# Margins in the plan of a hybrid encoder layer, and another spacing of its weight preparation

## The chip, the core and the metric

The kernel runs on one core of a Trainium2 chip, as one program with one launch. The metric is the time of that program on the device in microseconds (us); less is better. Before the change it is 2629.53 us, the median of three runs (2627.81 to 2630.4). The engines of the core run side by side, each its own queue of instructions in order, and wait for each other through semaphores: TensorE (PE, matrix products into eight PSUM banks), VectorE (DVE), ScalarE (ACT), GpSimd (POOL) and SyncE (SP, which issues most of the DMA transfers and all of the transposing ones).

## The reference

One encoder layer is applied to two requests, of 4096 and of 2048 tokens, 1024 wide, with the same weights.

```python
hn = rms_norm(x, norm_g)
proj = hn @ w_in                                   # 1024 -> 3072
na_q, na_k, na_v, na_g, wq, wk, wv, wg, mq, mg = jnp.split(proj, points, axis=-1)
ya = neighbourhood_attention(qa, ka, va, rpb) * jax.nn.silu(na_g)   # 6 heads, 8 x 16 window on a grid 64 wide
yb = windowed_gqa(qb, kb, vb, sink) * jax.nn.silu(wg)               # 6 heads, |t - s| <= 128
yc = memory_attention(qc, km, vm) * jax.nn.silu(mg)                 # 4 heads over 256 memory tokens
y = jnp.concatenate([ya, yb, yc], axis=-1) @ w_out
return x + y
```

Queries and keys of all three groups are normalised per head before the scores. The inputs are float32.

## The kernel before

Tokens are worked on in **superblocks** of 256 (24 of them: 16 of the first request, 8 of the second), each of two blocks of 128. Every product is made of float16 pairs, a high and a low part of each factor, so one projection of a block onto 384 columns is 24 matrix products (`proj`, L305).

[...] The **first pass** is the neighbourhood attention, the **second** the windowed and the memory attention, and the output projection. For a block of the first pass:

- x is loaded (L507), normalised (L524, DVE) and turned by TensorE in two halves into a PSUM bank each (L534, label `xT`); the halves are stored as float16 pairs (L544 ACT, L549 DVE).
- three projections follow (L308, L309, L311; labels `pga`, `pgb`, `pgv`). Queries and keys go to a float32 buffer and are squared (L672, L673 ACT), summed (L710 DVE), turned into a factor (L315 to L317 POOL) and multiplied by it (L717 DVE, label `nrm`); keys also by their gain (L722 POOL, label `kg`).
- TensorE turns queries (after `nrm`) and keys (after `kg`) into a bank each (L737, label `qT`, two tasks a block).

Then, for each superblock and each of three pairs of heads: scores (L936, label `qk`, into four banks at once), the reading of the four banks with bias and row minimum (L961 DVE, label `ttr`), exponentials (L971 ACT), reciprocal (L977, L978), probabilities as float16 pairs (L997 ACT, L1006 DVE), four transposing DMAs issued by SP (L1017), and the products with the values (L1033, label `pv`).

The PSUM banks are divided: two for projections (`pj`), four for turning and scores (`sc`), two for value products (`po`). A block of scores needs all four of `sc`, a turning one of them.

During the first pass the weights of the second are **prepared** as well, in 24 pieces and twice over: a first time each piece is loaded (L823) and its row maxima are taken (L828 DVE); a second time it is loaded again, split into a float16 pair (L855 ACT, L860 DVE) and stored to DRAM (L867), from where the second pass loads it. Lines L809 and L815 set at which superblock a piece becomes due.

**What sets the order.** No order is written out. All work is added as tasks to a plan (`Plan`, L63), each with an engine, an estimated duration, dependencies, a priority (made of the superblock's number and an offset by label, `SHIFT`), buffers that it takes (`acq`) and gives back (`rel`). `Plan.run` plays the tasks through on estimated times: whenever an engine is free it takes the ready task of least priority whose buffers are there, and the order in which it takes them is the order in which the instructions are issued. The chip then runs each engine's queue in that order at its own times. So an estimate in the plan makes no instruction wait by itself; it decides what stands before what.

A task is ready when its last dependency is done in the plan, or `slack` us after that:

```python
def push(now, t):
    if t.slack > 0:
        at(now + t.slack, READY, t)
    else:
        heapq.heappush(ready[t.eng], (t.prio, t.idx, t))
```

Of the kernel before, what the change touches and what calls it, by code (L numbers as in the profile page):

```python
# [41 lines left out]


class Task:
    __slots__ = ("eng", "dur", "fn", "prio", "lat", "acq", "rel", "nd", "succ", "idx", "label", "slack", "xf", "start", "run", "need")

# [9 lines left out]
TIMES = {"tanh": 0.4, "sg": 0.37, "ev": 0.95, "vl2": 0.235, "red2": 0.9, "r8": 2.85, "nrm2": 1.15, "hi2": 0.89, "lo2": 1.0,  # L58
         "wrcp": 0.275, "mmx": 0.63, "mexp": 1.06, "mrcp": 0.23, "mhi": 0.6, "mlo": 0.86, "ym": 0.37, "yh": 0.34, "yl": 0.37,
         "yw": 0.23, "fin": 0.7}  # L60


class Plan:  # L63
# [11 lines left out]
    def add(self, eng, dur, fn, deps=(), prio=0.0, lat=None, acq=(), rel=(), label="", slack=0.0, xf=0.0):  # L75


        t = Task()
        t.eng = t.run = eng
        t.dur, t.fn, t.prio = TIMES.get(label, dur), fn, prio + SHIFT.get(label, 0.0)  # L80
        t.lat = {"pe": 0.2, "dve": 0.13, "act": 0.13, "pool": 0.16, "free": 0.01}.get(eng, 0.1) if lat is None else lat
        t.acq, t.rel, t.succ = tuple(acq), tuple(rel), []
        names = [a[0] if isinstance(a, tuple) else a for a in acq]
        t.need = tuple((a, names.count(a)) for a in dict.fromkeys(names))
        t.idx, t.label, t.xf, t.slack, t.start = len(self.tasks), label, xf, slack, None
        if label.endswith("T"):
            t.xf *= 1.5
        if eng == "sp" and xf > 0:
            t.dur = (0.63 if label.endswith("T") else 0.45) * round(dur / 0.1)
        ds = [d for d in deps if d is not None]  # L90
        t.nd = len(ds)
        for d in ds:
            d.succ.append(t)
        self.tasks.append(t)
        return t
# [21 lines left out]
    def run(self):  # L117
        avail = self.avail = dict(self.caps)
        ready = {t.eng: [] for t in self.tasks}
        busy = {}  # L120
        ev = []
        seq = 0

        def at(when, kind, t):
            nonlocal seq
            heapq.heappush(ev, (when, seq, kind, t))
            seq += 1

        def push(now, t):
            if t.slack > 0:  # L130
                at(now + t.slack, READY, t)
            else:
                heapq.heappush(ready[t.eng], (t.prio, t.idx, t))
        FREE, DONE, READY, MOVE = range(4)
        for t in self.tasks:
            if t.nd == 0:
                push(0.0, t)
        now = 0.0
        done = 0
        dma_free = 0.0  # L140
        while done < len(self.tasks):
            progress = True
            while progress:
                progress = False
                for e, q in ready.items():
                    if busy.get(e, 0.0) > now or not q:
                        continue
                    skipped = []
                    pick = None
                    while q and pick is None and len(skipped) < 25:  # L150
                        item = heapq.heappop(q)
                        if all(avail[a] >= n for a, n in item[2].need):
                            pick = item[2]
                        else:
                            skipped.append(item)
                    for s in skipped:
                        heapq.heappush(q, s)
                    if pick is None:
                        continue
                    progress = True  # L160
                    self.acquire(pick)
                    pick.start = now
                    self.emit(pick)
                    busy[e] = now + pick.dur
                    at(busy[e], FREE, pick)
                    if pick.xf > 0:

                        at(now + (0.71 if pick.label.endswith("T") else 0.53 if e == "sp" else pick.dur) + 0.65, MOVE, pick)
                        if pick.label.endswith("T"):
                            busy[e] = 1e9  # L170
                    else:
                        at(now + pick.dur + pick.lat, DONE, pick)
            if not ev:
                left = [t.label for q in ready.values() for _, _, t in q][:20]
                raise RuntimeError(f"no progress at {now}: {left} {avail}")
            now = ev[0][0]
            while ev and ev[0][0] <= now:
                _, _, kind, t = heapq.heappop(ev)
                if kind == READY:
                    heapq.heappush(ready[t.eng], (t.prio, t.idx, t))  # L180
                elif kind == MOVE:
                    dma_free = max(now, dma_free) + t.xf
                    at(dma_free + 0.95, DONE, t)
                    if t.label.endswith("T"):

                        busy[t.eng] = max(now, dma_free - 0.9)
                        at(busy[t.eng], FREE, t)
                elif kind == DONE:
                    done += 1
                    self.release(t)  # L190
                if kind == DONE or (kind == FREE and t.xf == 0):

                    for s in t.succ:
                        if (s.eng == t.eng and t.xf == 0) == (kind == FREE):
                            s.nd -= 1
                            if s.nd == 0:
                                push(now, s)
        self.length = now


def build(tc, A, out, seqs):
# [3 lines left out]
    NSB = sum(seqs)  # L205
# [200 lines left out]
    for s in range(len(seqs)):  # L406
        mkv_views(s, one("SM", f"mkvs{s}", [P, 2048], F16))
        for b in range(2):
# [5 lines left out]
                  prio=-18, xf=0.27, label="c")  # L414
    t_gk = pl.add("pool", 1.1, lambda: G.dma_start(out=gam.rearrange("p a d -> p (a d)"), in_=A["k_norm_g"].partition_broadcast(P)),
                  prio=-17, xf=0.27, label="c")
# [29 lines left out]
    for nm, c0, n, src, fl, pr, parts in (("a", 0, 384, w_in, "w1", -29.09, 4), ("b", 384, 384, w_in, "w1", -27.0, 2),  # L446
# [4 lines left out]
        for pt_ in range(parts):  # L451
            ks = slice(nk_ * pt_, nk_ * pt_ + nk_)

            def f_l(ks=ks, c0=c0, n=n, src=src, fl=fl):
                SY.dma_start(out=st[fl + "f"][:, ks, c0:c0 + n],
                             in_=src[P * ks.start:P * ks.stop, c0:c0 + n].rearrange("(k p) c -> p k c", p=P))
            t = pl.add("sp", 0.1, f_l, prio=pr, label="wload", xf=2.2 * n / 384 * nk_ / 4,
                       slack={"v": 12.77, "n": 19.0, "m": 38.18, "b": 5.95}.get(nm, 0.0))
# [13 lines left out]
        t = scale_tasks(nm, g2, g, ts + [tg2_], pr - 30, parts=parts if nm in 'abvnm' else 0)  # L472
# [152 lines left out]
    for bt, nm, kw, nr in (("bA", "A", 32, 11), ("bB", "B", 24, 12)):  # L625
# [5 lines left out]
        t = pl.add("sp", 0.2, f_b, [t_T1], prio=0.9, acq=["pf"], label="bias", xf=3.0)  # L631
# [13 lines left out]
    for gs_ in range(NSB):  # L645
        s, g, n = sbs[gs_]
        for blk in range(2):
# [3 lines left out]
            def xT_alloc(gs_=gs_, blk=blk):  # L651
                if blk == 0:
# [5 lines left out]
                           label="xst", slack=9.0, xf=1.46)  # L658
# [18 lines left out]
            for key, nn, o in (("a", 384, 0), ("b", 384, 384)):  # L677
                t = ([t_xT] + list(t_p.values()))[-1]
                ew = 2 if nb == 0 else NK
                for k0 in range(0, NK, ew):  # L680
# [6 lines left out]
                                  prio=pr - 2, acq=["raw", "sq"] if key == "a" else [], rel=[("pj", key, nb)], label="ev" + key)  # L687
            t_p["v"] = pl.add("pe", 24 * (384 / 2.4 + 2.5) / 1000, mk_pg("v", 384), [t_p["b"]] + t_w["v"],
                              prio=pr, acq=[("pj", "v", nb)], label="pgv")
# [116 lines left out]


    pieces = [(nm, kk) for nm in "tgo" for kk in range(NK)]
    step = max(NSB - 8.5, 0.5) / (2 * len(pieces))  # L809
    prep = {}  # L810
    last = {}
    for ps_ in range(2):
        for i, (nm, kk) in enumerate(pieces):

            k_ = min(int(3.0 + (ps_ * len(pieces) + i) * step), NSB - 1)  # L815
            pr = k_ + 0.8
            n = W2[nm]
            src = A["w_out"][kk * P:(kk + 1) * P, :] if nm == "o" else w_in[kk * P:(kk + 1) * P,
# [828 lines left out]
```

## Time and profile before

| | before |
|---|---|
| runs, median (lowest to highest) | 2629.53 us (2627.81 to 2630.4) |
| the profiled execution | 2628.94 us |
| its span, first to last instruction | 2627.1 us |
| mean granted TensorE clock | 0.988 of full speed |

All times in the following are of that one profiled execution, in us from the start of its span. A row that groups instructions gives the line and engine, the operation, what it writes and reads, their shapes and count, then busy time, and idle time before it with what ended that. In a list of waits stand total us, number of times and the longest. In a row by time the idle time just before an instruction stands in brackets with what ended it. In a row by stretches stand, for each engine, busy us and (x) instructions, then the granted TensorE clock as a share of full speed, the busy share of the 16 DMA engines, and GB/s. Matmuls are pipelined and their ends modelled, so rows of one line overlap a little.

### The profile page before, as it was taken

How to read it: one execution, taken by the hardware profiler on the slowest of the kernel's cores; microseconds unless marked ns; L12 is line 12 of the kernel's file. 1: busy time of each engine (PE TensorE's matmuls, PEld its weight loads, DVE VectorE, ACT ScalarE, POOL GpSimd, SP SyncE). 2: the span in 40 equal slices, each digit the busy share in tenths (PEclk: the TensorE clock that was granted, in tenths of full speed). 3: DMA queues.
4: the chain of work that ended last, by engine and by line, in shares of the span. 5: the costliest groups of instructions: out<-in, count | busy, mean ns of one | idle time of the engine just before them, and what ended most of it. 6: DMA issues, size and time to landing. Idle time of an engine off the chain costs nothing.

```text
span 2627.1 us, 58284 instructions
## 1 busy us (share of the span) xinstructions
PE 2530.8 (96%) x22056; PEld 1589.0 (60%) x22056; DVE 1879.4 (72%) x5283; ACT 1247.3 (47%) x3553; POOL 523.4 (20%) x690
## 2 busy tenths in 40 slices
PE   6999998999999999987999999999999999999999
PEld 3666676666676666654555555555555555555555
DVE  6467776776776676676887777777777867777775
ACT  7455655566665665653444333333333433333432
POOL 2453232424243423220000000010001000000000
PEclk9999999999999999988999999999999999999999
DMA  5477777777979976896666566656655645566554
GB/s 197 150 174 174 164 164 162 169 178 195 190 187 219 208 145 153 172 224 138 146 139 125 120 132 130 129 123 124 127 119 119 131 118 130 127 137 129 123 108 111
DMA packets 732218, 394.56 MB, mean 150 GB/s; under 512 B 645344, under 2 KB 685056, under 8 KB 731296
## 3 DMA queue, kind: packets, MB, share of 16 engines
q1 hardware_dynamic: 718368, 346.59, 61.8%
q0 software_dynamic: 13568, 44.25, 4.7%
q8 instruction: 172, 2.82, 0.5%
q14 instruction: 110, 0.90, 0.1%
HBM read 153.72 MB, written 80.74 MB: 89 GB/s over the span
## 4 chain that ended last, share of the span: by engine, by line
PE 62%; DMA 2%; DVE 1%; SPq 1%; ACT 0%; issue 0%; POOL 0%; DVEq 0%; ACTq 0%; POOLq 0%
PE bank L308 7%; PE bank L1537 6%; PE bank L311 6%; PE bank L309 6%; PE bank L1538 6%; PE bank L1539 6%; PE bank L1241 4%; PE bank L1243 4%; PE bank L1242 4%; PE bank L1278 3%; PE bank L1364 3%; DMA pt<-phl 1%; PE bank L1455 1%; PE bank L1389 1%; PE bank L1033 1%; PE bank L936 1%
## 5 line engine op out<-in xcount | busy, mean ns | idle before, releaser
L308 PE MATMUL bank<-w,xT 128*128 128x384 f16 x1152 | 384.0, 334 | 3.3 <-ACT sq L673 2.2
L309 PE MATMUL bank<-w,xT 128*128 128x384 f16 x1152 | 382.8, 333 | 1.2 <-DVE w L370 1.2
L1329 ACT ACTIVATE pf<-pf,sm 128x384 f32<-128x384 f32 (+1 forms) x288 | 172.6, 599 | 289.1 <-DVE sm L1323 288.6
L1537 PE MATMUL bank<-wo,yT 128*128 128x512 f16 x768 | 291.5, 380 | 0.0
L1538 PE MATMUL bank<-wo,yT 128*128 128x512 f16 x768 | 291.1, 379 | 0.0
L1539 PE MATMUL bank<-wo,yT 128*128 128x512 f16 x768 | 291.1, 379 | 0.0
L315 POOL TENSOR_TENSOR r<-r,wA 128x12 f32<-128x12 f32 x48 | 10.4, 217 | 1275.9 <-DVE r L1194 1275.9
L317 POOL TENSOR_TENSOR r<-r,mhalf 128x12 f32<-128x12 f32 (+1 forms) x100 | 226.5, 2265 | 7.8
L311 PE MATMUL bank<-w,xT 128*128 128x384 f16 x1152 | 211.5, 327 | 0.0
L971 ACT ACTIVATE pf<-pf,sm 128x288 f32<-128x288 f32 (+3 forms) x288 | 155.6, 541 | 88.5 <-DVE sm L961 81.9
L1346 DVE SCALAR_TENSOR_TENSOR phl<-pf,sm,phl 128x384 f16<-128x384 f32 (+1 forms) x288 | 174.4, 606 | 8.6
L1006 DVE SCALAR_TENSOR_TENSOR phl<-pf,sm,phl 128x288 f16<-128x288 f32 (+3 forms) x288 | 152.2, 564 | 29.7 <-ACT phl L997 29.0
L1323 DVE CUSTOM_DVE_ANT_0 pf<-bank,wtab,nsink 128x384 f32<-128x384 f32 (+1 forms) x288 | 162.5, 600 | 6.4 <-PE bank L1278 6.3
L308 PEld LDWEIGHTS <-xT 128*128 128x128 f16 x1152 | 115.2, 100 | 83.8 <-issue 14.3
L309 PEld LDWEIGHTS <-xT 128*128 128x128 f16 x1152 | 115.0, 100 | 75.5 <-issue 9.9
L997 ACT ACTIVATE phl<-pf,sm 128x288 f16<-128x288 f32 (+3 forms) x288 | 144.5, 547 | 31.0 <-DMA pt<-phl 14.7
L311 PEld LDWEIGHTS <-xT 128*128 128x128 f16 x1152 | 113.1, 98 | 75.4 <-issue 1.4
L777 PE MATMUL bank<-xT,wn 128*128 128x256 f16 x576 | 157.3, 273 | 0.3 <-DVE sgn L792 0.3
L779 PE MATMUL bank<-xT,wn 128*128 128x256 f16 x576 | 157.0, 273 | 0.0
L778 PE MATMUL bank<-xT,wn 128*128 128x256 f16 x576 | 157.0, 273 | 0.0
L1177 ACT ACTIVATE raw<-bank 128x448 f32<-128x448 f32 x96 | 47.0, 490 | 221.2 <-PE bank L311 215.9
L1411 ACT ACTIVATE pf<-bank,smm 128x256 f32<-128x256 f32 x192 | 88.2, 481 | 125.3 <-DVE smm L1405 125.3
(281 smaller groups left out, 6063.2 us busy)
## 6 DMA issues: line engine op xcount, KB each, us to landing
xTd<-xT POOLq DMA_DIRECT2D x48, 512.0 KB, 4.3
out<-xr SPq DMA_DIRECT2D x48, 512.0 KB
xx<-in_x_prompt SPq DMA_DIRECT2D x32, 512.0 KB
xr<-in_x_prompt SPq DMA_DIRECT2D x32, 512.0 KB
x<-xTd SPq DMA_DIRECT2D x24, 512.0 KB
w<-xTd SPq DMA_DIRECT2D x24, 512.0 KB
vd<-vhl POOLq DMA_DIRECT2D x48, 192.0 KB, 3.0
va<-vd SPq DMA_DIRECT2D x48, 192.0 KB
```

Of the source, the lines that this page charges most:

```text
L308: T.matmul(ps, xt[:, kk], wh[:, kk, cols], start=(kk == 0), stop=False)
L309: T.matmul(ps, xt[:, kk], wl[:, kk, cols], start=False, stop=False)
L311: T.matmul(ps, xt[:, NK + kk], wh[:, kk, cols], start=False, stop=(kk == NK - 1))
L317: G.tensor_tensor(out=r, in0=r, in1=mhalf[:, 0:n], op=ALU.pow)
L777: T.matmul(pv, wh, x[:, :, kk, :], start=(kk == 0), stop=False)
L778: T.matmul(pv, wh, x[:, :, NK + kk, :], start=False, stop=False)
L1323: V.tensor_tensor_reduce(out=pf[:, 0:nk], in0=bank("sc", "w", u)[:, 0:nk], in1=st["wtab"][:, h, c0:c0 + nk], scale=-1.0, scalar=nsink[:, h ...
L1329: S.activation(out=pf[:, 0:nk], in_=pf[:, 0:nk], func=AF.Exp, scale=-1.0, bias=sm[:, 0:1], accum_out=sm[:, 1:2])
L1346: V.scalar_tensor_tensor(out=phl[:, nk:2 * nk], in0=st["pfw", u][:, 0:nk], scalar=st["smw", u][:, 3:4], in1=phl[:, 0:nk], op0=ALU.mult, op ...
L1537: T.matmul(ps, yT[:, 0, ts_], st["wo0"][:, c, cs], start=(ci == 0), stop=False)
L1538: T.matmul(ps, yT[:, 0, ts_], st["wo1"][:, c, cs], start=False, stop=False)
L1539: T.matmul(ps, yT[:, 1, ts_], st["wo0"][:, c, cs], start=False, stop=(ci == 7))
```

## The change

Three labels get a margin in the plan. A turning of queries or keys (`qT`) and a value product (`pv`) become ready 1.5 us later than their last dependency is done in the plan; a reading of scores (`ttr`) gives its bank back 1.5 us after it is done there. Nothing is added to what the engines do: the number of tasks, their instructions, bytes and buffers are the same.

The preparation of weights is spaced anew. `NSB` is 24 and there are 24 pieces. Before, 48 steps of 15.5/48 of a superblock begin at 3.0; now the first round begins at 2.0 with steps of 18.5/72, and the second round takes two such steps a piece.

```diff
+LATE = {"qT": 1.5, "pv": 1.5}
+KEEP = {"ttr": 1.5}
...
-        t.idx, t.label, t.xf, t.slack, t.start = len(self.tasks), label, xf, slack, None
+        t.idx, t.label, t.xf, t.start = len(self.tasks), label, xf, None
+        t.slack, t.keep = slack + LATE.get(label, 0.0), KEEP.get(label, 0.0)
...
-        FREE, DONE, READY, MOVE = range(4)
+        FREE, DONE, READY, MOVE, GIVE = range(5)
...
+                elif kind == GIVE:
+                    self.release(t)
                 elif kind == DONE:
                     done += 1
-                    self.release(t)
+                    if t.keep > 0:
+                        at(now + t.keep, GIVE, t)
+                    else:
+                        self.release(t)
...
-    step = max(NSB - 8.5, 0.5) / (2 * len(pieces))
+    step = max(NSB - 5.5, 0.5) / (3 * len(pieces))
...
-            k_ = min(int(3.0 + (ps_ * len(pieces) + i) * step), NSB - 1)
+            k_ = min(int(2.0 + (i if ps_ == 0 else len(pieces) + 2 * i) * step), NSB - 1)
```

The lines of the kernel move by 5 to 13 with it: L308, L311, L737, L1033, L1241 before are L320, L323, L749, L1046, L1254 after.

What it does to the order shows on TensorE at two places. The first is a block in the middle of the first pass, the 37th, at 856 to 863 us of the trace of before. The rows are those around its two turnings of queries (the first `ident,raw` row) and keys (the second), before:

```order
L311 MATMUL bank_63<-w_307,xT 128x384
L737 MATMUL bank_68<-ident,raw 128x2x4x16 x3
L737 MATMUL bank_65<-ident,raw 128x128 x3
L1033 LDWEIGHTS va
L1033 MATMUL bank_69<-pt,va 64x8x16
```

and after, where the dots stand for the rest of a value product and of a projection:

```order
L323 MATMUL bank_64<-w_307,xT 128x384
L749 MATMUL bank_65<-ident,raw 128x2x4x16 x3
L1046 LDWEIGHTS va
L1046 MATMUL bank_69<-pt,va 64x8x16
...
L320 MATMUL bank_63<-w_307,xT 128x384
...
L323 MATMUL bank_63<-w_307,xT 128x384
L749 MATMUL bank_66<-ident,raw 128x128 x3
```

The keys' turning has moved behind the value product and a whole projection; the queries' turning stands where it stood.

The second place is the end of the first pass on TensorE, from its last scores (`ring,qT`, 64x256) to the first gates of the second pass (the row that reads `x_15604,wn` or `x_15572,wn`). Projections of the second pass write 128x448. Shown is the first product of each group, before:

```order
L936 MATMUL bank_66<-ring,qT 64x256
...
L308 MATMUL bank_63<-w_16526 128x448
...
L1033 MATMUL bank_69<-pt,va 64x8x16
...
L308 MATMUL bank_64<-w_16526 128x448
...
L1033 MATMUL bank_70<-pt,va 64x8x16
...
L1241 MATMUL bank_64<-x_15604,wn_16898 128x256
```

Here one projection, one value product, two projections and three value products lie between the last scores and the gates. After:

```order
L949 MATMUL bank_65<-ring,qT 64x256
...
L320 MATMUL bank_63<-w_16407 128x448
...
L1046 MATMUL bank_69<-pt,va 64x8x16
...
L1254 MATMUL bank_63<-x_15572,wn_16788 128x256
...
L1046 MATMUL bank_70<-pt,va 64x8x16
...
L1254 MATMUL bank_63<-x_15572,wn_16788 128x256
```

The last scores are now followed by two projections and three value products; then come two gates, the last value product, and further gates. One projection has moved ahead of the last scores.

More of the change, by code (lines that the diff above doesn't have):

```diff
@@ L44 @@
 class Task:
-    __slots__ = ("eng", "dur", "fn", "prio", "lat", "acq", "rel", "nd", "succ", "idx", "label", "slack", "xf", "start", "run", "need")
+    __slots__ = ("eng", "dur", "fn", "prio", "lat", "acq", "rel", "nd", "succ", "idx", "label", "slack", "xf", "start", "run", "need", "keep")
 SHIFT = {"bE": 0.02, "c": 1.22, "eva": 0.26, "evb": -0.01, "exp": -0.1, "g2": 1.94, "hi": 0.3, "kg": -1.0,
```

## The prediction

> **What bounds the kernel now.** First the page as a whole: the span, the share of each engine, and the strips of the span in 40 slices.
>
> ```profile
> span 2627.1 us, 58284 instructions
> PE 2530.8 (96%) x22056; PEld 1589.0 (60%) x22056; DVE 1879.4 (72%) x5283; ACT 1247.3 (47%) x3553; POOL 523.4 (20%) x690
> ...
> PE   6999998999999999987999999999999999999999
> ...
> PEclk9999999999999999988999999999999999999999
> DMA  5477777777979976896666566656655645566554
> ```
>
> TensorE has work for 2530.8 of 2627.1 us and the next engine, VectorE, for 1879.4. So the end is set by TensorE's own matmuls plus the 96.3 us in which it stands idle, and only those 96 us (and time at a lower clock) can be won by another order. The next view, the busy time in four stretches, says where they are.
>
> ```profile
> core 0: us, PE busy (x) PEld busy (x) DVE busy (x) ACT busy (x) POOL busy (x), PEclk, DMA share, GB/s
> 0.00:150.00 150.00, 122.83 (x759) 78.53 (x760) 81.83 (x197) 84.93 (x167) 61.66 (x91) 0.97 0.50 169
> 150.00:1140.00 990.00, 947.97 (x10891) 659.55 (x10890) 700.03 (x1868) 604.85 (x1572) 332.67 (x459) 0.99 0.80 178
> 1140.00:1230.00 90.00, 67.35 (x561) 44.47 (x560) 57.63 (x170) 34.73 (x109) 13.87 (x15) 0.85 0.80 189
> 1230.00:2627.00 1397.00, 1392.66 (x9851) 806.50 (x9847) 1039.93 (x3049) 522.84 (x1707) 115.20 (x126) 1.00 0.59 126
> ```
>
> Idle are 27.2 us in the start, 42.0 us in the first pass (neighbourhood attention), 22.6 us at the hand-over to the second pass, and 4.3 us in all 1397 us after it. The second pass is full: nothing is to be had there, and its order changes only in its first superblocks. The list of who waited for whom on TensorE names the 42.0 us of the first pass:
>
> ```profile
> PE bank L1033 <- DMA pt<-phl: 12.9, 9, 3.7
> PE bank L534 <- DVE sm L961: 10.4, 6, 3.5
> PE bank L737 <- POOL raw L722: 6.8, 6, 2.2
> PE bank L737 <- DVE raw L717: 6.3, 6, 3.1
> ...
> PE bank L936 <- DVE xT L549: 1.6, 2, 1.3
> PE bank L737 <- DVE sm L961: 0.8, 1, 0.8
> ```
>
> The columns are total us, times, and the longest. Value products (L1033) wait 12.9 us for turned probabilities; the turning of queries and keys (L737) waits 13.9 us in 13 places for their norm and gain; the turning of x (L534) waits 10.4 us and scores (L936) 1.6 us for a score bank.
>
> A wait costs more than its length, because the clock halves after it. Five stretches of the granted clock (the third number from the right):
>
> ```profile
> 189.50:192.90 3.40, 3.40 (x43) 1.94 (x43) 2.14 (x5) 2.60 (x6) 1.32 (x2) 0.50 0.88 271
> 404.50:407.90 3.40, 3.40 (x13) 1.95 (x14) 2.13 (x6) 3.40 (x9) 0.00 (x0) 0.50 0.13 26
> 452.30:455.70 3.40, 3.40 (x16) 2.77 (x16) 1.97 (x8) 3.40 (x10) 0.00 (x0) 0.50 0.83 135
> 810.70:817.50 6.80, 5.44 (x50) 3.13 (x50) 3.65 (x6) 3.37 (x6) 5.55 (x8) 0.50 1.15 295
> 861.90:865.30 3.40, 3.40 (x40) 2.27 (x40) 2.80 (x6) 1.85 (x5) 3.20 (x7) 0.50 0.89 149
> ```
>
> At 0.50 each 3.4 us do the work of 1.7. These five lose 10.2 us, and the mean of 0.99 over 990 us agrees with about 10. Two of them (404, 452) follow waits of L534, two (189, 810) waits of L1033, one (861) a wait of L737.
>
> **The margin at queries and keys.** The stretch at 856 us shows what is to be removed: two turnings back to back, each late.
>
> ```profile
> 856.75 1.46 PE L311 MATMUL bank<-w,xT 128*128 128x384 f16 x8
> 858.75 0.55 PE L737 MATMUL bank<-ident,raw 128*128 128x128 f32 x3 [0.54 <-DVE raw L717]
> 861.42 0.55 PE L737 MATMUL bank<-ident,raw 128*128 128x128 f32 x3 [2.12 <-POOL raw L722]
> 861.90 1.49 PE L1033 MATMUL bank<-pt,va 128*64 128x128 f16 x32
> ```
>
> The first order excerpt shows this place: after the change a value product (1.49 us here) and a projection stand between the two turnings. The projection's length is in the next fence: 448.00 - 444.09 = 3.91 us. So the second turning comes 5.4 us later in TensorE's work and its wait of 2.12 us is covered. In all 48 blocks the pair is now split by at least one other piece of work (41 were back to back). Counted over the rows of the order at lengths like these, the first turning stands at least 8.0 us of work behind the projection it needs, where it stood 7.5 at the least. The waits for POOL's gain (6.8 us) should nearly all go. Of the 7.1 us for VectorE the longest, 3.1, can lose only about 1.5. I take 10 of 13.9 us; the bounds are 4 (the margin is eaten by later norms) and 13.9.
>
> **The margin at value products.** 12.9 us in 9 waits is 1.4 us in the mean, longest 3.7. A product that comes 1.5 us later clears the mean wait and leaves 2.2 of the longest. But scores are pushed back as well, so the work between a pair's scores and its product grows in some places and shrinks in others. I take 8 of 12.9; bounds 0 and 12.9.
>
> **The margin at score banks.** It clears L936: 1.6 us. For L534 I take nothing of 10.4 us. These rows of TensorE and VectorE show why:
>
> ```profile
> 443.13 1.02 PE L936 MATMUL bank<-ring,qT 64*64 64x256 f16 x48
> 444.09 0.34 PE L308 MATMUL bank<-w,xT 128*128 128x384 f16 x1
> ...
> 448.00 0.60 PE L534 MATMUL bank<-ident,xx 128*128 128x128 f32 x4
> 452.12 1.19 PE L534 MATMUL bank<-ident,xx 128*128 128x128 f32 x5 [3.52 <-DVE sm L961]
> ...
> 403.17 0.82 DVE L828 TENSOR_REDUCE sc_gmx<-xw 128x1 f32<-128x640 f32 x1 [5.97 <-DMA xw<-in_w_in]
> ...
> 450.41 1.22 DVE L828 TENSOR_REDUCE sc_omx<-xw 128x1 f32<-128x1024 f32 x1 [4.37 <-DMA xw<-in_w_out]
> 451.55 0.51 DVE L961 CUSTOM_DVE_ANT_0 pf<-bank,bA 128x352 f32<-128x352 f32 x1
> ```
>
> VectorE stood 4.37 us before a weight maximum (L828) whose load had not landed, and the scores' reading (L961), which frees the bank, was queued behind it; the row at 403 is the same ahead of the half-clock stretch at 404. Scores and turning of x lie one projection (3.91 us) apart, and in the new order they mostly still do; 1.5 us more in the plan was already inside that distance. What could end this wait is another place of the maximum, which the new step gives, by luck. Bounds 0 and 10.4.
>
> **The clock.** With those waits the half-clock stretches at 189, 810 and 861 should mostly go: 1.7 + 3.4 + 1.7 = 6.8 us. I take 4, bounds 0 and 10.2. [...]
>
> **The weight step.** Pieces of the first pass over the later weights come every 18.5/72 = 0.26 superblocks instead of 15.5/48 = 0.32, those of the second every 0.51 instead of 0.32. No instruction and no byte is added. When the largest pieces of the second pass are split shows in this row (ns shortest/median/longest, then first and last start in us):
>
> ```profile
> L855 ACT ACTIVATE xhl<-xw,sc_ogs x8: 1132/1148/1150, 792.0 to 917.6; 128x1024 f16<-128x1024 f32 x8
> ```
>
> That is where the DMA strip has its two 9s side by side (788 to 919 us); these pieces come half as often there now. Its gain is contained in the L1033 term; alone I price it at 0. Bounds: minus 5 (waits like that at 452 are gone) to plus 10 (the denser maxima make two more, each 3.5 us and 1.7 of clock).
>
> **The hand-over.** Here the change can cost. Waits between 1140 and 1230 us, and the end of the first pass on TensorE:
>
> ```profile
> PE bank L1033 <- DMA pt<-phl: 8.8, 4, 4.4
> PE bank L1364 <- DMA pt<-phl: 4.4, 3, 2.7
> PE bank L1389 <- DVE sm L1323: 4.1, 3, 2.0
> ...
> 1136.60 1.68 PE L311 MATMUL bank<-w 128*128 128x448 f16 x8
> 1141.57 1.68 PE L311 MATMUL bank<-w 128*128 128x448 f16 x8
> 1143.18 0.95 PE L1033 MATMUL bank<-pt,va 128*64 128x128 f16 x33
> 1148.48 0.77 PE L1033 MATMUL bank<-pt,va 128*64 128x128 f16 x16 [4.36 <-DMA pt<-phl]
> ```
>
> Before, three projections of the second pass lay between the last scores and the last value products; now two (second order excerpt). One such projection is 1141.57 - 1136.60 = 4.97 us here, gap-free. The first of the last products meets its probabilities that much earlier, and nothing is late behind it but the other products. Against this, two gates are put ahead of the very last product. Scores and mask work of the second pass are also re-ordered up to about its fourth superblock. I take plus 5; bounds minus 5 (the gates cover it) and plus 15 (the whole of it, again at half clock as PEclk 0.85 shows for this stretch).
>
> **Sum.** 10 + 8 + 1.6 + 4 - 5 = 18.6 us off. The profiled execution took 2628.94 us (span 2627.1 and 1.8 around it), 0.6 under the median of 2629.53. 2628.9 - 18.6 = 2610.
>
> **The rivals.**
> - *All waits go* (chance 0.08). Also those for a bank, and the hand-over stays as it is: 42.0 + 10.2 = 52 us at most, less what starts anew; about 2585. For it: every wait of the first pass is at one of the three places or comes from a bank. Against: the bank waits come from late loads.
> - *The clock does not come back* (0.05). The waits shrink but the rest is enough to halve the clock as often: 2628.9 - 14.6 = 2614. [...]
> - *The waits only move* (0.22). An order has no time in it: scores are pushed back as well, and what stood before a product stands before the next scores. For it: between scores and product the work is the same in many superblocks. The change does not do what it says, within 8 us of 2626; a third of it faster by over 0.2%.
> - *Slower at the hand-over* (0.14). The last products run into their probabilities, 5 us each for the last two, and into the first window products (L1364 and L1389, 8.5 us now), which stretches the half clock as well. It decides from the point where the hand-over loses more than the first pass wins: at the lower bounds that is 4 + 1.6 won against 10 and some 4 of half clock lost, 2628.9 + 8.4 = 2637.
> - *The denser maxima* (0.07). The step of 0.26 superblocks makes VectorE wait for loads more often just ahead of a scores' reading. Two of 24 reach TensorE now; at six it is 4 x (3.5 + 1.7) = 21 us against 18.6: 2631.
>
> **How the numbers follow.** Forecast 0.44, all waits 0.08, clock 0.05, move 0.22, hand-over 0.14, maxima 0.07. A measurement of this kernel can tell about 0.2%, 5.3 us, from no change. Faster by more: 0.44 + 0.08 + 0.05 and a third of 0.22, 0.64. Slower by more: the hand-over and some of the maxima and the moves, 0.20. Within: 0.16. The range for 8 in 10 leaves out most of "all waits" below and the worst of the hand-over above: 2588 to 2637.
>
> **What would show it.** In the first pass the waits of the turning of queries and keys for POOL fall below 2 us and for VectorE below 3; those of the value products for turned probabilities to about 5; the bank waits of x stay, but at other times, each behind a weight maximum on VectorE; half-clock stretches fall to two or three. Between the end of the first pass and the first output product the idle time rises by about 5 us. The DMA strip has no 9 near 850 us. The forecast is wrong if the idle time of the first pass stays above 35 us, or if the hand-over loses over 15.

## Result and profile after

| | before | after |
|---|---|---|
| median | 2629.53 us | 2651.94 us |
| lowest to highest | 2627.81 to 2630.4 | 2645.99 to 2655.26 |
| ratio of after to before (95% interval) | | 1.0083 (1.0069 to 1.0097) |
| profiled execution, its span | 2628.94, 2627.1 us | 2645.99, 2644.2 us |

The change made the kernel 22.4 us slower; 2610 was forecast, and the range ended at 2637. The profiled execution of after is the lowest of its runs, so the traces show 17.1 us of the difference. Of the experiments below, one execution of e8_tenth (6069 us) and one of h1_pool_before (2926 us) were far slower than all others; the ratios leave them out, and without them the two medians are 2633.74 and 2613.05 us.

The page of after, answering to the first fence of the prediction:

```profile
span 2644.2 us, 58237 instructions
PE 2536.9 (96%) x22056; PEld 1593.6 (60%) x22056; DVE 1878.6 (71%) x5283; ACT 1247.6 (47%) x3553; POOL 524.1 (20%) x690
...
PE   6999988999999999987999999999999999999999
...
PEclk9999999999999999988999999999999999999999
DMA  5466977887888986886766656665555645566654
```

TensorE's work is the same 22056 matmuls. Its busy time grew by 6.1 us, about what the longer time at half clock makes of the same work (worked out below), and its idle time by 11.0 (from 96.3 to 2644.2 - 2536.9 = 107.3). The busy time by stretches says where (us of the stretch, then busy us of each engine, then clock); the stretches end some 15 us later than those of before, as the work does:

```profile
0.00:150.00 150.00, 123.77 (x745) 79.28 (x746) 82.35 (x196) 86.81 (x170) 61.84 (x94) 0.97 0.50 171
150.00:450.00 300.00, 273.94 (x3063) 191.99 (x3061) 203.82 (x540) 165.62 (x437) 96.98 (x137) 0.97 0.78 165
450.00:750.00 300.00, 288.17 (x3480) 202.61 (x3479) 219.69 (x584) 191.50 (x483) 93.93 (x131) 0.99 0.86 181
750.00:1155.00 405.00, 391.92 (x4399) 269.50 (x4398) 277.90 (x749) 246.95 (x649) 144.09 (x191) 0.98 0.86 178
1155.00:1250.00 95.00, 69.32 (x551) 45.24 (x551) 58.67 (x175) 35.91 (x118) 11.19 (x13) 0.82 0.69 175
1250.00:2644.00 1394.00, 1389.73 (x9826) 804.95 (x9824) 1036.13 (x3045) 520.86 (x1700) 116.09 (x126) 1.00 0.59 127
```

The first pass (150 to 1155) idles 51.0 us where it idled 42.0; the hand-over 25.7 where it idled 22.6; start and second pass are as before. Of the first pass the stretch from 150 to 450 took nearly all: 26.1 us of idle time. In before it is this row, with 14.4:

```profile
150.00:450.00 300.00, 285.61 (x3329) 200.97 (x3327) 215.84 (x580) 179.83 (x477) 99.74 (x142) 0.98 0.77 168
```

The waits of TensorE in the first pass of after:

```profile
PE bank L1046 <- DMA pt<-phl: 18.0, 8, 6.3
PE bank L362 <- DVE sc_gis L356: 7.0, 1, 7.0
PE bank L949 <- DVE xT L561: 5.1, 9, 1.2
PE bank L749 <- DVE sm L974: 4.1, 3, 2.1
PE bank L749 <- DVE raw L729: 4.1, 3, 2.6
...
PE bank L949 <- DVE ring L315: 2.2, 2, 1.5
PE bank L362 <- DVE sc_tis L356: 2.2, 1, 2.2
PE bank L546 <- DVE sm L974: 1.5, 1, 1.5
PE bank L546 <- DVE ring L315: 0.9, 1, 0.9
PE bank L749 <- POOL raw L734: 0.9, 2, 0.6
```

The waits at the turning of queries and keys (L749) and of x (L546) are shorter. But those of value products (L1046) are longer, scores (L949) wait for other things than before, and a line that had no wait in the first pass of before stands second: L362, the small product that makes the scale of a weight out of its maxima. The two longest waits, by time, with what stood before them on SP and VectorE:

```profile
303.14 2.83 SPq L816 DMA_DIRECT2D va<-vd  x4
306.01 8.50 SPq L1030 DMA_TRANSPOSE pt<-phl  x2
...
318.38 2.08 PE L1046 MATMUL bank<-pt,va 128*64 128x128 f16 x47 [6.25 <-DMA pt<-phl]
...
347.91 2.63 SPq L816 DMA_DIRECT2D va<-vd  x4
350.64 0.46 SPq L836 DMA_DIRECT2D xw<-in_w_in  x1
...
360.13 0.82 DVE L841 TENSOR_REDUCE sc_gmx<-xw 128x1 f32<-128x640 f32 x1 [7.08 <-DMA xw<-in_w_in]
...
361.41 0.58 PE L362 MATMUL bank<-sc_gis,ones 128*128 128x1 f32 x2 [6.96 <-DVE sc_gis L356]
```

At 303 four value loads (L816) went out ahead of the turnings of probabilities; two of those took 8.50 us on SP (a median one takes 1.29), and the product behind them was 6.25 us late. At 360 VectorE stood 7.08 us before a weight maximum whose load had not landed, and TensorE with it; that load (L836, at 350.64) had been issued right behind four more value loads. Half clock stands at both, 6.8 and 10.2 us of it:

```profile
316.40:323.20 6.80, 4.82 (x99) 3.98 (x99) 1.62 (x4) 0.92 (x2) 0.00 (x0) 0.50 1.07 311
357.40:367.60 10.20, 6.19 (x21) 3.15 (x22) 6.20 (x29) 3.46 (x10) 0.00 (x0) 0.50 0.57 93
...
862.50:869.30 6.80, 6.12 (x32) 3.15 (x32) 3.84 (x10) 3.37 (x9) 3.97 (x6) 0.50 0.98 237
...
sum 37.40, PE 30.04 PEld 18.07 DVE 19.54 ACT 15.37 POOL 11.40; mean PE 4.29 PEld 2.58 DVE 2.79 ACT 2.20 POOL 1.63
```

The sum is that of all seven half-clock stretches of the first pass; before, there were 23.8 us (the five that the prediction showed, and 3.4 us at 322.6), with TensorE at work for 22.4 of them. VectorE's waits for the loads of the weight maxima grew as well, from 32.4 us (11.6 + 11.4 + 9.4) to 56.0:

```profile
DVE sc_gmx L841 <- DMA xw<-in_w_in: 20.7, 4, 9.4
DVE sc_tmx L841 <- DMA xw<-in_w_in: 20.6, 6, 8.4
DVE sc_omx L841 <- DMA xw<-in_w_out: 14.7, 4, 5.4
```

### The profile page after: what moved, and what is told of

Same layout as the page of the kernel before. It is cut to its first block, busy times and chain, and to the rows that moved or that the text cites. A ratio compares the mean times of both kernels' runs of the same rounds, so it can differ in the third digit from the quotient of the medians.

```text
span 2644.2 us, 58237 instructions
## 1 busy us (share of the span) xinstructions
PE 2536.9 (96%) x22056; PEld 1593.6 (60%) x22056; DVE 1878.6 (71%) x5283; ACT 1247.6 (47%) x3553; POOL 524.1 (20%) x690
## 4 chain that ended last, share of the span: by engine, by line
PE 58%; DVE 2%; DMA 1%; ACT 1%; POOL 0%; issue 0%; SPq 0%; DVEq 0%; ACTq 0%; POOLq 0%
PE bank L1550 6%; PE bank L1551 6%; PE bank L1552 6%; PE bank L320 6%; PE bank L321 6%; PE bank L323 6%; PE bank L1254 4%; PE bank L1256 4%; PE bank L1255 4%; PE bank L1291 3%; PE bank L1377 3%; PE bank L1468 1%; PE bank L1402 1%; DMA pt<-phl 1%; PE bank L1046 0%
## 5 line engine op out<-in xcount | busy, mean ns | idle before, releaser
L320 PE MATMUL bank<-w,xT 128*128 128x384 f16 x1152 | 384.9, 335 | 3.4 <-ACT sq L685 3.1
L323 PE MATMUL bank<-w,xT 128*128 128x384 f16 x1152 | 213.3, 329 | 0.0
L1019 DVE SCALAR_TENSOR_TENSOR phl<-pf,sm,phl 128x288 f16<-128x288 f32 (+3 forms) x288 | 157.2, 583 | 23.3 <-ACT phl L1010 22.4
L320 PEld LDWEIGHTS <-xT 128*128 128x128 f16 x1152 | 115.6, 100 | 82.3 <-issue 14.7
L323 PEld LDWEIGHTS <-xT 128*128 128x128 f16 x1152 | 113.9, 99 | 77.4 <-issue 4.5
```

Source lines behind the costliest of these rows:

```text
L320: T.matmul(ps, xt[:, kk], wh[:, kk, cols], start=(kk == 0), stop=False)
L323: T.matmul(ps, xt[:, NK + kk], wh[:, kk, cols], start=False, stop=(kk == NK - 1))
```

## The experiments

All of them compute the same as the kernel before. "Step" is the new spacing of the weight pieces, "margins" the other two edits. Ratios are to runs of the kernel before on the same chip.

| label | what it is | median us | ratio (95% interval) |
|---|---|---|---|
| e1_step_only | new step, no margin | 2637.72 | 1.0023 (1.0013 to 1.0033) |
| e2_margins_only | margins, old step | 2649.26 | 1.0067 (1.0047 to 1.0088) |
| e3_scale_margin | after, and L362 8 us later in the plan | 2658.36 | 1.0103 (1.0084 to 1.0121) |
| e4_no_bank_margin | old step, two margins (no bank margin) | 2657.99 | 1.0097 (1.0075 to 1.0119) |
| e5_bank_only | old step, bank margin alone, 0.8 us | 2654.01 | 1.0088 (1.0072 to 1.0105) |
| e6_value_only | old step, value margin alone | 2635.58 | 1.0022 (1.0012 to 1.0032) |
| e7_turn_only | old step, margin of queries and keys alone | 2642.14 | 1.0047 (1.0032 to 1.0062) |
| e8_tenth | old step, all margins 0.1 us | 2635.35 | 1.0020 (1.0009 to 1.0031) |
| f1_loads_spread | after, value loads among the turnings | 2664.69 | 1.0136 (1.0119 to 1.0154) |
| f2_maxima_later | after, maxima later on VectorE | 2637.17 | 1.0024 (1.0009 to 1.0039) |
| f3_both_after | f1 and f2 together | 2656.45 | 1.0106 (1.0080 to 1.0132) |
| f4_both_before | the same two on before | 2696.82 | 1.0261 (1.0236 to 1.0285) |
| g1_maxima_before | before, maxima later | 2614.26 | 0.9934 (0.9918 to 0.9951) |
| g2_maxima_margins | e2, maxima later | 2642.23 | 1.0042 (1.0027 to 1.0056) |
| g3_maxima_value | e6, maxima later | 2615.49 | 0.9939 (0.9925 to 0.9954) |
| g4_loads_on_pool | after, value loads issued by POOL | 2628.75 | 0.9999 (0.9985 to 1.0013) |
| h1_pool_before | before, value loads issued by POOL | 2613.07 | 0.9940 (0.9924 to 0.9955) |
| h2_pool_maxima_before | before, both moves | 2615.94 | 0.9953 (0.9936 to 0.9971) |

### The parts of the change

The first runs take the change apart. e1 keeps the new step and empties the tables of margins; e2 does the opposite:

```diff
-LATE = {"qT": 1.5, "pv": 1.5}
-KEEP = {"ttr": 1.5}
+LATE = {}
+KEEP = {}
```

> The new step of the weight preparation alone, no margin anywhere. Theory A (the step loses the time: its denser maxima stop VectorE for loads, and the scale product L362 on TensorE waits behind them, 7.0 + 2.2 us and 10.2 us of half clock in the changed kernel): 2645 to 2660, with waits of L362 for sc_gis or sc_tis on TensorE. Theory B (the margins lose it, by putting scores and value products in worse places): within 5 us of 2629.5.

> The three margins alone, with the old step. Theory A: 2610 to 2625, waits of L749 and L1046 in the first pass shorter than before, no wait of L362 for sc_gis. Theory B: 2640 to 2655, with waits of L1046 and L949 as in the changed kernel.

The step alone cost 8 us and the margins alone 19 (8 + 19 = 27 against 22 together): both parts cost, and the margins more. e2 lies in the range of theory B, e1 between the two theories. e2 shows where the margins lose: its value products wait longer than in before, although each has a margin of 1.5 us.

```profile
PE bank L1046 <- DMA pt<-phl: 21.8, 10, 6.9
PE bank L749 <- DVE raw L729: 14.5, 8, 5.0
```

e3 is after with the scale product held back in the plan, for the wait of 6.96 us:

```diff
-LATE = {"qT": 1.5, "pv": 1.5}
+LATE = {"qT": 1.5, "pv": 1.5, "sc2": 8.0}
```

> The changed kernel, and in the plan the scale product of a weight (sc2, L362) becomes ready 8 us later, so that other work stands before it on TensorE. If its waits and the half clock behind them are 14 us of the loss, as the trace of the changed kernel adds up (9.2 us of waits and 10.2 us at half clock): 2634 to 2642, no wait of L362 for sc_gis or sc_tis above 1 us. If these waits only show a late VectorE that something else would meet: no change, 2646 to 2655, with the wait at another line.

The wait went and the kernel became 6 us slower still, which neither theory had: one number in the plan had drawn the whole order anew. So taking a wait out by a margin does not test what that wait costs. e4 leaves out the margin at score banks (`KEEP = {}`, old step):

> Old step, margins at the turning and at value products only, none at score banks. If the bank margin is what pushes scores back: waits of L949 for VectorE as before the change (1.8 us) and a time below the margins alone by 3 us or more. If it is harmless: within 4 us of the margins alone.

Value products then waited only 9.0 us, but the kernel lost 28, more than either theory allowed. Next, each margin alone, and all of them at a length that can cover nothing (old step in all four):

```diff
e5  +LATE = {}                         +KEEP = {"ttr": 0.8}
e6  +LATE = {"pv": 1.5}                +KEEP = {}
e7  +LATE = {"qT": 1.5}                +KEEP = {}
e8  +LATE = {"qT": 0.1, "pv": 0.1}     +KEEP = {"ttr": 0.1}
```

> The old weight step; of the three margins only the one at score banks, at 0.8 us instead of 1.5 (with 1.5 alone the plan finds no order). Theory 'lead': bank waits fall a little, scores are pushed back, shortest distance to the value product stays 14.5; 2627 to 2637. Theory 'redrawn': 2635 to 2660.

> The old weight step; of the three margins only the one at value products (1.5 us). In the written order the work between a pair's scores and its value product grows to 21.4 us in the mean and 17.9 at the least (before 20.0 and 14.3; with all margins 20.0 and 15.4), since nothing pushes the scores back. Theory 'lead': the margin at value products fails in the full change because the other margins push the scores back as far; alone it works, so the first-pass waits of value products for turned probabilities fall from 12.9 to about 5 us and the time is 2615 to 2628 us. Theory 'redrawn': any order other than that of before meets new waits, the size of a margin decides nothing; the waits of value products fall, others rise by as much or more, and the time is 2635 to 2660.

> The old weight step; of the three margins only the one at the turning of queries and keys (1.5 us). Theory 'lead': the second turning moves from 10.3 to 13.1 us behind its projection, the 13.9 us of waits there fall below 4, but scores go back and value products lose lead (shortest 13.9 us): their waits rise from 12.9 to about 25; 2630 to 2640. Theory 'redrawn': 2635 to 2660, with the new waits at places that have no margin in common (score banks, weight maxima, value products).

> The old weight step; all three margins at 0.1 us instead of 1.5, which is too short to cover any wait of a microsecond or more. The written order is redrawn all the same: the second turning of queries and keys stands 11.9 us behind its projection (before 10.3, with 1.5 us 13.8). Theory 'lead' (margins of 1.5 us do the harm, by their size): within 5 us of before, 2625 to 2635. Theory 'redrawn' (the order of before is a fortunate one, any other costs): as the full margins, 2637 to 2660.

By their times, "lead" fell at e5, e6 and e7, where "redrawn" was right in sign and size; e8 came out at the edge of "lead", 0.2% (5 us) above before. One mark of "lead" did come in e7: value products waited 23.8 us, where it had about 25. Margins of 0.1 us, which cover no wait of a microsecond, cost 5 us; one margin alone costs 5, 12 or 24, all three 19, and two of them 28. What an order costs does not follow the size or the number of the margins. The value margin alone did at its place what it was to do, and this is what stood there then (first-pass waits of e6):

```profile
PE bank L546 <- DVE sm L974: 11.7, 7, 3.7
PE bank L949 <- DVE sm L974: 6.4, 3, 5.6
PE bank L1046 <- DMA pt<-phl: 5.0, 3, 2.3
PE bank L749 <- DVE sm L974: 4.9, 3, 2.0
PE bank L949 <- DVE xT L561: 3.8, 6, 1.3
```

The waits of products went from 12.9 to 5.0 us as hoped, and TensorE's waits for VectorE from 19.9 to 34.4 (all rows of that list together).

### The two queues, without a new order

To see what single waits cost, the other runs keep the plan's order and move a few instructions when they are issued. f1 issues the four value loads one behind each of the next four turnings; f2 issues each weight maximum up to eight pieces of VectorE's work later:

```diff
 # f1
     def emit(self, t):
+        if t.label == "vld":
...
+            self.hold = [lambda cb=cb: t.fn(cbs=[cb]) for cb in range(4)]
+            return
         t.fn()
+        if t.label == "pT" and self.hold:
+            self.hold.pop(0)()
 # f2
     def emit(self, t):
+        if t.label == "wpm":
+            self.hold, self.left = [t.fn], 8
+            return
+        if self.hold:
+            self.left -= t.eng == "dve"
+            if self.left == 0 or t.label in ("wpl", "sc1"):
+                self.hold.pop()()
         t.fn()
```

> The full change, its order kept on every engine; only the four value loads of a superblock (L816), which stand together on SP, are issued one behind each of the next four turnings of probabilities. Theory 'queue': the long waits of the full change for turned probabilities (6.3, 3.3 and 2.6 us at 312, 985 and 860 us) arise because the turnings stand behind those loads on SP; they go, the first-pass waits there fall from 18 to about 8, and with the half clock behind them the time falls by 10 to 16 us, to 2636 to 2642. Theory 'only moves': the turnings are as late as before for other loads, or another engine is late next; within 5 us of 2652.

> The full change, its order kept on every engine but VectorE, where each weight maximum (L841) stands up to eight pieces of work later. Theory 'queue': VectorE waits 56 us for loads of the maxima, with the readings of scores queued behind; this falls below 25, TensorE's first-pass waits for VectorE fall from 28 to about 15 us, and the time falls by 8 to 18 us, to 2634 to 2644. Theory 'only moves': the waits on VectorE shrink but TensorE's waits for it stay above 23 us; within 5 us of 2652.

> The full change with both: value loads one behind each turning, and the maxima up to eight pieces later on VectorE. Theory 'queue': the two add up, 2618 to 2634, so most of what the change lost is regained without touching a margin. Theory 'only moves': 2640 to 2657.

> The kernel before (old step, no margin, its order), with the value loads one behind each turning and the maxima up to eight pieces later on VectorE. Theory 'queue': of the first pass's 42 us of waits those behind value loads (3.8 us at 807) and behind maxima (L534, 10.4 us) go, with some half clock; 2612 to 2624. Theory 'fortunate order': before has few such meetings to lose, and the moved pieces make new ones; 2625 to 2640.

f2 fits "queue" by its time: VectorE's waits for these loads fell from 56.0 to 9.2 us, and 15 us were gained. TensorE's waits for VectorE fell from 28.1 to 19.3 us, less than it asked, and the wait at the scale product stayed (7.0 us in after, 6.7 in f2). f1 went the wrong way. Its wait of 6.25 us was gone, but products now waited for the loads themselves, which they had done in neither kernel (f1, then f4):

```profile
PE bank L1056 <- DMA pt<-phl: 15.9, 12, 3.8
PE bank L1056 <- DMA va<-vd: 8.9, 5, 3.3
```

```profile
PE bank L1064 <- DMA pt<-phl: 38.0, 26, 4.4
PE bank L1064 <- DMA va<-vd: 24.6, 18, 3.4
```

f4 and g1 below differ in the place of these loads alone: 2696.82 against 2614.26, so that place is worth 83 us there. On the changed order it cost 13 us (f1) and 19 us (f3 against f2). f1, f3 and f4 thus say that the meeting of loads and turnings on SP matters, not that it made the difference. The next runs apply each move to both kernels; g4 and h1 take the loads off SP altogether:

```diff
-                SY.dma_start(out=va[0:4 * kw, cb, :], in_=vsrc[:, CB_KC0[cb]:CB_KC0[cb] + kw, :])
+                G.dma_start(out=va[0:4 * kw, cb, :], in_=vsrc[:, CB_KC0[cb]:CB_KC0[cb] + kw, :])
```

> The kernel before, its order kept on every engine but VectorE, where each weight maximum stands up to eight pieces of work later. VectorE's waits for the loads of the maxima fall from 32 to below 8 us. Theory 'maxima': the re-drawn order made these waits reach TensorE, while in the order of before they mostly did not; so the gain here is small, 0 to 7 us, 2622 to 2631. Theory 'common cost': both kernels have it and the difference of 22 us stays; the gain is as in the full change, 12 to 17 us, 2613 to 2619.

> All three margins of 1.5 us, the old weight step, and each weight maximum up to eight pieces later on VectorE. Without the last it took 2649. Theory 'maxima': VectorE's 45 us of waits for loads go below 15, and the time comes to 2629 to 2638. Theory 'redrawn': value products wait 21.8 us here for turned probabilities, with which the maxima have nothing to do; 2642 to 2650.

> Only the margin at value products, the old weight step, and each weight maximum up to eight pieces later. Without the last it took 2636, its value products waiting 5 us instead of 12.9 and VectorE making TensorE wait 34 us instead of 20. Theory 'maxima': the 34 us fall to about 18 and the margin's own gain shows: 2612 to 2622, below the kernel before. Theory 'redrawn': 2628 to 2638.

> The full change, its order kept; only the value loads (L816) are issued by POOL instead of SP, at the same place of the order. Theory 'queue': the waits of value products behind such a load (6.3, 3.3 and 2.6 us at 312, 985 and 860 us) go; POOL issues for some 4 us more in each superblock and its gain (L734) comes later, which the margin at queries and keys covers; 2638 to 2646. Theory 'only moves': the turnings are as late as before, or the gain makes the turning of queries and keys wait 10 us or more; 2647 to 2665.

> The kernel before, its order kept; only the value loads are issued by POOL instead of SP. In the full change this took 23 us off. Theory 'loads': the re-drawn order put value loads right ahead of turnings that TensorE waits for, the order of before mostly not (one long wait, 3.8 us at 807, stands behind one); the gain here is 0 to 8 us, 2623 to 2631, and the two kernels come within 5 us of each other. Theory 'common cost': 15 to 25 us are gained here too, 2606 to 2616, and the change stays about 20 us slower with the loads away. Theory 'gain late': without the margin at queries and keys POOL's issuing makes the turning wait for the gain, from 6.8 us up to 15 or more; 2631 to 2645.

> The kernel before with both moves: value loads issued by POOL, and each weight maximum up to eight pieces later on VectorE. The maxima alone took it to 2614. If the two add up, with 0 to 8 us from the loads, 2606 to 2614; with a common cost of the loads of 15 to 25 us, 2590 to 2600; if POOL's gain is late instead, 2615 to 2630.

**The maxima** are a common cost: moving them gave 17 us on before and 15 on after, and the gap between the two stayed at 2637.17 - 2614.26 = 22.9 us. g2 gained 7 of the 11 to 20 that "maxima" asked and lies in the range of "redrawn". g3 landed where "maxima" had put it, but not for its reason: it and g1 differ in the value margin alone and came out 1.2 us apart, within the spread of either. With VectorE's waits for the loads of the maxima gone (0.6 us in g1, 32.4 before), that margin is worth nothing, and its order, which cost 5 us in e6, costs nothing either.

**The loads on SP** were worth 23 us on after and 16 on before, so by the medians they too are mostly a common cost, as one theory had it; g4 came out faster than both of its theories allowed. The gap between the two kernels fell from 22.4 to 15.7 us, by about as much as the intervals of the four ratios leave open. The traces of one execution each say where the rest is. The stretches of g4, then of h1:

```profile
150.00:1130.00 980.00, 949.60 (x10938) 663.34 (x10937) 704.47 (x1868) 604.88 (x1566) 395.25 (x547) 0.99 0.86 180
1130.00:1230.00 100.00, 71.29 (x599) 46.62 (x594) 61.20 (x185) 38.16 (x124) 11.18 (x13) 0.81 0.71 172
```

```profile
150.00:1125.00 975.00, 944.80 (x10900) 659.12 (x10898) 704.31 (x1868) 606.28 (x1573) 394.99 (x547) 0.99 0.81 181
1125.00:1215.00 90.00, 68.98 (x574) 45.44 (x573) 59.24 (x179) 35.36 (x112) 13.63 (x15) 0.85 0.80 192
```

Idle in the first pass are 30.4 and 30.2 us: the 9.0 us by which the changed order idled more are gone. The half clock of the first pass is equal too, 20.4 us in each. Most of what is left of the gap (2623.1 - 2610.2 = 12.9 us of span) is the hand-over: 28.7 us idle against 21.0, and 37.5 us of half clock against 27.3. So on these two traces the loss of the first pass arises only together with the value loads on SP, and the loss at the hand-over does not. With the maxima moved instead, the first passes stay apart (f2 idles 995 - 951.8 = 43.2 us there, g1 978 - 945.2 = 32.8).

The waits did not simply go where "queue" had put them. At the three products that it named, 6.25, 3.25 and 2.61 us of after became 3.15, 3.95 and 0.62 in g4, so only some of that waiting hangs on the place of the value loads. The wait at L362 fell from 7.0 to 0.9 us, though nothing was moved on VectorE: the weights' loads stand on SP as well, and VectorE's waits for them fell from 56.0 to 39.2 us in g4, and from 32.4 to 12.5 in h1. In h1 the waits of value products hardly changed (12.9 to 11.9 us); there the turning of x (10.4 to 6.2) and of queries and keys (13.9 to 9.6) waited less. By which step on the way that happens was not tried.

The best are h1 and g1, both on the kernel before, at 2613 and 2614 us (0.6% below it). The two moves do not add up: h2 took 2616. Its waits for POOL's gain are only 3.5 us, so that theory is not the reason; h1 alone had already taken most of VectorE's waits for the maxima away, which fits that the second adds nothing; it was not tried further.

## Why the prediction was wrong

Its account of the first pass, against what after shows (us of waits before and after; a change below zero is a gain):

| step | forecast | before, after | change |
|---|---|---|---|
| turning of queries and keys, L737/L749 | -10 | 13.9, 9.1 | -4.8 |
| value products, L1033/L1046 | -8 | 12.9, 18.0 | +5.1 |
| scores, L936/L949 | -1.6 | 1.8, 7.6 | +5.8 |
| turning of x, L534/L546 | 0 | 10.4, 2.4 | -8.0 |
| scale products, L350/L362 | none | 0, 9.2 | +9.2 |
| projections and gates | none | 2.6, 4.0 | +1.4 |
| sum of waits | -19.6 | 41.6, 50.3 | +8.7 |
| half clock, half of TensorE's work in it | -4 | 11.2, 15.0 | +3.8 |
| hand-over, idle and half clock | +5 | | +5.5 |

For the last row: idle +3.0, and TensorE's work in the half-clock stretches from 16.8 to 21.8 us, half of which is 2.5. Half, because the 128x384 products of a projection start 0.32 us apart in the half-clock stretch at 404.5 of before (405.58, 405.90) and 0.16 us apart right behind it (408.05, 408.21). The prediction took half of the whole length of such stretches (10.2 us in five of them); where TensorE idles within one, as at 810, that counts the idle time twice. Counted as in the table, the rows sum to 8.7 + 3.8 + 5.5 = 18.0 us; 0.9 is won in the start, which leaves the 17.1 us of span.

- **The step that failed** is the sum itself: "10 + 8 + 1.6 + 4", rows of the old order's list of waits taken off its time. Off the waits and the half clock of the first pass 23.6 us were to come; 12.5 were added. A margin in this plan does not take a wait out; it draws another order for all engines, which meets waits of its own. The nearest rival, "the waits only move", named this, but priced it at no change. The runs show that the moves were not neutral: nine redrawn orders (after, and e1 to e8) all came out slower, by 5 to 28 us. That the order of before is a fortunate one fits this; why no redrawn one was better is not shown.
- *Queries and keys.* Right for POOL (6.8 to 0.9, "below 2" was asked), wrong for VectorE (7.1 to 8.2, "below 3").
- *Value products.* Wrong in sign in the full change, right alone: the margin took 7.9 us off in e6 for a forecast of 8. With this margin and none at score banks the products waited 5.0 and 9.0 us (e6, e4), with both margins 21.8 and 18.0 (e2, after). The count ahead of e6 fits that: the work between a pair's scores and its product is 20.0 us in the mean before, 21.4 with the value margin alone, and 20.0 again with all three, so the other margins take back what this one gives. The prediction had named this ("scores are pushed back as well") and still took the 8.
- *Turning of x.* Said to stay "each behind a weight maximum", gained by luck; it waits 8.0 us less in after, and f2 and g1 show that the place of the maxima was worth 15 to 17 us. I had taken that as out of reach of the change and priced it at zero.
- *Weight step.* Priced at 0 with bounds of -5 and +10; e1 measured +8. Of the DMA strip's pair of 9s one is gone; the other stays in the slice from 859 to 925 us, where none was forecast. *Denser maxima* grew from 32 to 56 us of VectorE's waits, but f2 against g1 shows that they do not make the difference.
- *The clock.* Seven stretches of the first pass and 37.4 us, where two or three stretches were forecast. A wait of 2.61 us stands at 6.8 us of half clock, at 862.5. Not every wait has the clock halved after it, as the prediction put it: before, waits of up to 3.12 us passed at full clock; the last section has the list.
- *The hand-over.* Right in size, 5.5 us for a forecast of 5, but by luck: the last products were to wait longer for their probabilities, and they wait 8.1 us where they waited 8.8. What grew are the waits of the window scores of the second pass (L1278, now L1291, 0.3 to 5.5 us) and of its gates (L1243, now L1254 and L1256, 0.5 to 3.5); which step of the new order makes them wait was not tried. The rows of before, then those of after:

```profile
PE bank L1243 <- DMA wgc<-w2dg: 0.5, 1, 0.5
PE bank L1278 <- DVE sm L1323: 0.3, 1, 0.3
```

```profile
PE bank L1046 <- DMA pt<-phl: 8.1, 4, 3.3
...
PE bank L1291 <- DVE sm L1336: 3.9, 2, 2.8
PE bank L1256 <- DMA wgc<-w2dg: 2.2, 1, 2.2
PE bank L1291 <- ACT pf L1424: 1.6, 1, 1.6
...
PE bank L1254 <- DVE vw L1201: 1.3, 1, 1.3
```

Of the two marks that the prediction set for its own failure one was met (first-pass idle above 35 us) and one not (the hand-over lost less than 15).

What stays open: which meetings cost e4, e5 and e7 their 12 to 28 us was not tried one by one, and g4 and h1 are one trace each.

## What to carry to other kernels

Where a planner makes the order, do not subtract waits from the time for a change of its numbers: first draw the order anew with a change that can do nothing (0.1 us; here that moved the time by 5 us) and see how far the time moves; only a gain beyond that speaks for the number. To learn what a wait costs, keep the order and move only the instruction that stands in the way. Before giving a waiting consumer more margin, look at what its producer queues behind: here four loads stood ahead of the turnings on one queue, and issuing them from another engine halved the longest wait of value products of the changed kernel (6.25 to 3.15 us) and gave 16 us on the kernel before.

## What the runs showed of the hardware

- Issuing the value loads from POOL instead of SP gave 16 us (h1) though it adds 66 us of busy time to POOL (589.7 against 523.4); TensorE's waits for POOL did not grow (4.8 us in h1, 6.8 before).
- Interleaving the same loads with the turnings on SP was worse than issuing the four together: f4 against g1, 83 us; on the changed order 13 (f1) and 19 us (f3 against f2). That products then waited for the loads themselves (24.6 us in 18 times) is shown; why a load that is issued between two turnings lands so late was not tried.
- In the first pass of before, six stretches had a granted clock of 0.50. They begin at 189.5, 322.6, 404.5, 452.3, 810.7 and 861.9 us; that at 810.7 lasted 6.8 us, the others 3.4. The waits of TensorE that ended just before or within them were, in this order, 3.67, 1.99, 3.19, 3.52, 1.62 with 2.17, and 2.12 us. Waits of 3.12 us (to 921.42), 2.19 (to 232.00 and to 640.54) and 2.04 (to 937.73) went with the full clock, 1.00 throughout from 918 to 926, 228 to 236, 637 to 645 and 934 to 943. In after, a half-clock stretch at 606.5 has only waits of 0.81, 0.29 and 0.32 us just ahead of it (to 604.19, 604.78 and 605.98). So on these two traces the length of a single wait does not tell whether half clock follows it; what decides is not shown.
